# Gate columns of two hybrid mixers made in a strand of their own, five accumulators for the first head, and RMS norms summed per token

## The chip, the core and the metric

The kernel runs on one core of a Trainium2 chip. The metric is the device time of one execution in microseconds (us); a kernel's time is the median over its runs.

## What is computed

A stack of six blocks on one sequence of 512 tokens ("l") of width 1024, with a context of 256 tokens ("c") beside it in the first layer. First a two-layer network: layer 0 has a mixer (a scan and a spatial gate) and a convolutional ffn, layer 1 an mLSTM and an ffn. Then two hybrid mixers. Everything is float32. Each block begins with an RMS norm over the 1024 channels of a token. In the reference, cut to what matters here:

```python
def rms_norm(x, w):
    xf = x.astype(jnp.float32)
    y = xf * lax.rsqrt(jnp.mean(xf * xf, axis=-1, keepdims=True) + EPS)
    return (y * w.astype(jnp.float32)).astype(x.dtype)

def hybrid_mixer(h, ...):
    proj = h @ w_in
    qkv, z_a, a_lg, b_lg, cf_val, cf_glu, z_b, gate_lg = jnp.split(proj, pts, axis=-1)
    qkv = jax.nn.silu(depthwise_conv_centred(qkv, qkv_conv_w))     # 5 taps
    ...
    g = -jnp.exp(a_log) * jax.nn.softplus(a_lg + dt_bias)          # 2 directions x 4 heads
    beta = jax.nn.sigmoid(b_lg)
    o_fwd = gated_delta_chunked(q, k, v, g[:, :, 0], beta[:, :, 0])
    ...                                                            # the same backward
    y_a = (o_fwd + o_bwd, normed, times silu(z_a)) @ w_dn_out
    y_b = (a 31-tap convolution of cf_val * sigmoid(cf_glu), normed, gated) @ w_cf_out
    y = gate[:, :, 0] * y_a + gate[:, :, 1] * y_b
    return y @ w_out

for l in range(DEPTH):
    x = x + hybrid_mixer(rms_norm(x, norm_w[l]), ...)
```

`gated_delta_chunked` needs, for each head, direction and chunk of 64 tokens, the cumulated g, its exponentials and beta. These few numbers per token are the "gate columns" of the title.

## The kernel before

Activations are held channel-major: a tile is 128 channels by 512 tokens, eight tiles (KD = 8) make the width. A gemm (`gemm_tile`, `mmacc`) takes the weights in slabs of 128 output channels and runs three matmuls per input tile (L344, L347, L348: high times high, high times low part, low times high), 24 per slab of 128, into one PSUM bank. On ScalarE (L80) and VectorE (L81) each slab's weights are split into the two parts, `wh` and `wl`. A set of banks and buffers is an `Env`: its `mm` list is the accumulators that gemms take in turn, its `ps` list the banks of all else.

The norms. `normed` runs six times: at the start, before the first ffn, before the mLSTM, before the second ffn, before hybrid 0 and before hybrid 1. Where a block's output y has to be added first (the second to the fifth), it norms y, adds it to x tile by tile (L476, L470), squares each new x tile on ScalarE (L395), and sums the squares over channels on TensorE. `wide_sum` (L425) does this with one matmul per tile: a 128x128 weight of ones, the 512 tokens moving, so that every row of the bank holds the sums of all tokens. `wide_rms` reads the diagonals of that bank with one VectorE instruction per 128 tokens (L433, each with a read of its accumulator), adds epsilon (L435), raises to the power -1/2 on GpSimd (L437), and spreads the result over 128 rows by four transposes (L388). Only then can VectorE write the normed tiles (L492, L485) that the next gemm reads. Records on TensorE come in twos for a float32 matmul: the 16 records of L425 in a norm are 8 tiles.

A hybrid mixer. `hybrid` first makes the 16 gate rows by a gemm (`gate_rows`, weights `gwh`), then the gate columns, then runs `gdn_proj` for heads 0 and 1: for each head four gemms in the order k, q, v, za, each into the next accumulator of `pro`, which has banks 0, 1 and 2. After each of k, q and v, VectorE adds four taps from the bank (L1794, after ScalarE's centre tap L1786); for k and q, ScalarE squares the result (`qsq`, L2017) and TensorE sums it (L374). za is a plain gemm with a silu. The fourth gemm of a head takes the first accumulator again. Heads run as background strands, generators that the main program steps by planned times ("due"): `head(a)` waits until its head's projections are there, then yields through `gdn_head`. The strands share TensorE with the gemms that follow: `cf_proj`, heads 2 and 3, the gate and z projections, the branch 1 gemms; then `K.drain()` runs out whatever is left of the heads, and the branch 0 gemms end the mixer. Within the planned order, the final order of each engine is set by a scheduler that simulates the program while it is built.

The lines that matter below: gate columns in L1814 to L1852 (`G` L1438, exponent and logarithm L1470 to L1472, L1819, L1820, the scan L1825, the transposes L1459, `eglT` L1849), projections L2003 to L2026, a head's chain L2124 to L2160, its output transposes L2188. In the changed kernel most helper lines come 2 or 3 earlier (L344 is L342, L374 is L372, L388 is L386, L1459 is L1456, L1794 is L1791) and those of `gdn_head` 9 later.

## Time and profile before

| | |
|---|---|
| median of 3 runs | 3421.62 us (3419.37 to 3433.52) |
| profiled execution | 3418.44 us, of which 3416.7 us are the span of the trace |
| TensorE (PE) busy | 3151.7 us, 92% of the span |
| VectorE (DVE), ScalarE (ACT), GpSimd (POOL) busy | 62%, 37%, 18% |
| mean granted TensorE clock | 0.953 of full speed |

The span runs from the first to the last instruction of the core. The granted clock is the share of full TensorE speed (2.4 GHz) that the chip gave: 1.00 is 2.4 GHz, 0.50 is 1.2 GHz, values between are stretches with both. PEld is TensorE's weight loading, which overlaps its matmuls (PE). A row of a timeline reads: start in us, duration in us, engine, line, operation, what is written <- what is read, partitions and shape, how many in the row, and in brackets how long the engine had been idle before and what released it. A row of waits reads: who waited, for whom, us in total, times, longest.

### The profile page before, as it was taken

The numbers are of one execution on the slowest core, as the hardware profiler recorded it, in microseconds if no ns is written. First come the engines' busy times: TensorE is split into PE (matmuls) and PEld (weight loads), VectorE is DVE, ScalarE is ACT, GpSimd is POOL, SyncE is SP. The second block draws the span as 40 slices with busy tenths as digits, with TensorE's granted clock in tenths as the row PEclk, the third lists the DMA queues.
The fourth block names the chain that finished last, engine by engine and source line by source line (L and its number), as shares of the span: only waits on it lengthen the run. The fifth ranks groups of instructions, "written<-read, shape, count | busy, mean of one in ns | idle before, by whom it ended". The sixth has DMA issues, their size and how long they took to land.

```text
span 3416.7 us, 61935 instructions
## 1 busy us (share of the span) xinstructions
PE 3151.7 (92%) x25042; PEld 2476.2 (72%) x25042; DVE 2122.4 (62%) x4318; ACT 1269.4 (37%) x2679; POOL 614.0 (18%) x762
## 2 busy tenths in 40 slices
PE   7999898888899999989888999988999899999988
PEld 4878676667688888868765888767667567766756
DVE  4444565645855555685666576677777666677665
ACT  4333343333432222364433332352433335233332
POOL 4111222211000000010010000005156000525500
PEclk8999998999999999999998999989999899999979
DMA  6432554431222222122222223232232343123332
GB/s 228 141 94 70 166 167 155 139 112 52 73 72 68 72 73 97 57 73 69 81 78 82 91 87 132 78 99 78 69 103 95 104 138 102 57 69 108 102 115 90
DMA packets 313570, 336.10 MB, mean 98 GB/s; under 512 B 26542, under 2 KB 259132, under 8 KB 313284
## 3 DMA queue, kind: packets, MB, share of 16 engines
q1 hardware_dynamic: 311172, 329.69, 30.0%
q8 instruction: 197, 3.23, 0.4%
q0 software_dynamic: 2112, 2.45, 0.3%
q14 instruction: 89, 0.73, 0.1%
HBM read 282.13 MB, written 49.94 MB: 97 GB/s over the span
## 4 chain that ended last, share of the span: by engine, by line
PE 61%; issue 18%; DVE 14%; ACT 3%; DMA 3%; POOL 0%; SPq 0%; DVEq 0%; POOLq 0%; ACTq 0%
PE mm L344 14%; PE mm L347 13%; PE mm L348 13%; DVE cfa L1794 3%; PE ps L739 2%; PE ps L748 2%; PE ps L1192 2%; DVE wl L81 2%; PE ps L1137 1%; PE ps L558 1%; PE ps L1719 1%; PE ps L2133 1%; DMA ld<-sp 1%; PE ps L2160 1%; PE ps L1701 1%
## 5 line engine op out<-in xcount | busy, mean ns | idle before, releaser
L344 PE MATMUL mm<-hl,wh 128*128 128x512 f32 (+1 forms) x3296 | 1249.6, 383 | 56.0 <-DVE qkv L1794 15.2
L347 PE MATMUL mm<-hl,wh 128*128 128x512 f32 (+1 forms) x3296 | 1225.8, 372 | 1.6 <-DVE hl L487 1.6
L348 PE MATMUL mm<-hl,wl 128*128 128x512 f32 (+1 forms) x3296 | 1218.5, 372 | 0.0
L344 PEld LDWEIGHTS mm<-hl,wh 128*128 128x128 f32 x3296 | 631.1, 192 | 192.8 <-issue 33.2
L348 PEld LDWEIGHTS mm<-hl,wl 128*128 128x128 f32 x3296 | 631.4, 192 | 114.6 <-issue 2.8
L347 PEld LDWEIGHTS mm<-hl,wh 128*128 128x128 f32 x3296 | 633.2, 192 | 106.3 <-DVE hl L487 3.4
L80 ACT ACTIVATE wh<-wr 128x512 fp32r<-128x512 f32 (+3 forms) x718 | 367.9, 561 | 704.2 <-PE mm L347 614.3
L81 DVE TENSOR_TENSOR wl<-wr,wh 128x512 fp32r<-128x512 f32 (+3 forms) x718 | 435.7, 640 | 230.1 <-ACT wh L80 205.2
L1372 DVE SCALAR_TENSOR_TENSOR cv<-mm,vecs,cv 128x441 f32<-128x441 f32 (+2 forms) x352 | 242.9, 692 | 94.3 <-ACT cv L1360 88.2
L1423 POOL MEMSET gwh<- 128x1024 f32 x3 | 2.9, 955 | 969.2 <-PE mm L347 969.2
L1794 DVE SCALAR_TENSOR_TENSOR cfa<-ld,vecs,cfa 128x497 f32<-128x497 f32 (+14 forms) x160 | 162.1, 1013 | 13.2 <-ACT cfa L1788 11.0
L1962 POOL TENSOR_SCALAR tap<-ld,vecs 128x498 f32<-128x498 f32 (+4 forms) x80 | 150.6, 1882 | 63.9 <-PE ps L2046 29.8
L1395 DVE TENSOR_TENSOR fy<-fy,mm 128x512 f32<-128x512 f32 x96 | 55.2, 577 | 126.3 <-PE mm L348 125.5
L1963 POOL TENSOR_TENSOR cfa<-cfa,tap 128x498 f32<-128x498 f32 (+4 forms) x80 | 112.1, 1401 | 5.3
L743 ACT ACTIVATE pad<-ps 128x256 f32<-128x256 f32 (+1 forms) x100 | 46.7, 468 | 155.5 <-PE ps L739 155.0
L2138 ACT ACTIVATE u<-ps,beT 64x128 f32<-64x128 f32 x128 | 46.2, 362 | 131.3 <-DVE u L2137 130.6
L1374 ACT ACTIVATE cv<-cv,vecs 128x256 f32<-128x256 f32 (+1 forms) x66 | 43.0, 652 | 132.1 <-DVE cv L1372 77.2
L749 DVE TENSOR_TENSOR cut<-cut,ps 128x256 f32<-128x256 f32 x120 | 49.3, 413 | 54.0 <-PE ps L748 53.2
L2137 DVE TENSOR_SCALAR u<-ps,kdT 64x128 f32<-64x128 f32 x128 | 44.5, 349 | 58.4 <-PE ps L2133 44.4
L1378 DVE TENSOR_TENSOR cv<-cv,mm 128x512 f32<-128x512 f32 x66 | 39.5, 599 | 65.5 <-ACT cv L1374 36.2
L425 PE MATMUL ps<-sq,one 128*128 128x512 f32 (+1 forms) x132 | 62.6, 609 | 15.8 <-ACT sq L395 13.7
L731 POOL TENSOR_TENSOR pad<-L,zm 128x512 f32<-128x512 f32 x40 | 54.4, 1360 | 113.4 <-PE ps L739 84.0
(479 smaller groups left out, 4418.9 us busy)
## 6 DMA issues: line engine op xcount, KB each, us to landing
...
```

Source lines behind the costliest of these rows:

```text
L80: nc.scalar.activation(h[:, q:e], src, AF.Copy)
L81: nc.vector.tensor_tensor(l[:, q:e], src, h[:, q:e].bitcast(F32), SUB)
L344: mm = nc.tensor.matmul(ps[:m, :n], wh[:, i, :m], H[:, :n], start=first and i == 0, stop=False)
L347: nc.tensor.matmul(ps[:m, :n], wh[:, i, :m], L[:, :n], start=False, stop=False)
L348: nc.tensor.matmul(ps[:m, :n], wl[:, i, :m], H[:, :n], start=False, stop=last and i == nk - 1)
L739: nc.tensor.matmul(ps[r, u * 64:u * 64 + 64], L[r, u], W[r, u], start=True, stop=True)
L748: nc.tensor.matmul(ps[r, u * 64:u * 64 + 64], X[r, u], Z[r, u], start=True, stop=True)
L1192: nc.tensor.matmul(ps[hs[h], d], lhsT(d, h), rhs(d, h), start=first and i == 0 and d == 0, stop=last and i == len(parts) - 1, skip_group_c ...
L1372: nc.vector.scalar_tensor_tensor(t3[:, ro, co], a3[:, ri, ci], tap(ky, kx, ff), t3[:, ro, co], MUL, ADD)
L1794: nc.vector.scalar_tensor_tensor(dst[:, a:b], src[:, a + o:b + o], taps[j], dst[:, a:b], MUL, ADD)
L1962: nc.gpsimd.tensor_scalar(x[:, a:b], src[:, a + o:b + o], taps[j], None, MUL)
L1963: nc.gpsimd.tensor_tensor(g[:, a:b], g[:, a:b], x[:, a:b], ADD)
```

## The change

Three things. (1) `wide_sum` becomes `token_sum`: each squared tile is the weight, 128 tokens at a time, and a single column of ones moves, so the bank gets one column of sums per 128 tokens, four matmuls (eight records) per 512-token tile. `wide_rms` becomes `token_rms`: one VectorE instruction reads these columns; the power and the four transposes stay. The constant `one2` goes. (2) In `hybrid` the gate columns become a generator in a background strand with banks 6 and 7, stepped at planned times; the heads wait for `cols` too. (3) Head 0's projections run with five accumulators, banks 0, 1, 2, 4 and 5; from head 1 on it is `pro` with three.

```diff
-    def wide_sum(self, ps, t, n, first, last):
-
-        self.nc.tensor.matmul(ps[:, :n], self.one2, t[:, :n], start=first, stop=last)
+    def token_sum(self, ps, t, n, first, last):
+
+        for i in range(n // P):
+            self.nc.tensor.matmul(ps[:, i:i + 1], t[:, i * P:(i + 1) * P], self.ones, start=first and i == 0,
+                                  stop=last, skip_group_check=True)
         self.free(t)
 
-    def wide_rms(self, ps, n):
-
-        c = self.tiny([P, n // P], name="dg")
-        for i in range(n // P):
-            junk = self.s128(name="junk")
-            self.line(self.nc.vector.scalar_tensor_tensor(junk, ps[:, i * P:(i + 1) * P], 1.0 / D, self.ident, MUL, MUL,
-                                                          accum_out=c[:, i:i + 1]))
-        self.line(self.nc.vector.tensor_scalar(c, c, EPS, None, ADD))
-        r = self.tiny([P, n // P], name="rs")
-        self.nc.gpsimd.tensor_tensor(r, c, self.mhalf[:, :n // P], ALU.pow)
+    def token_rms(self, ps, n):
+
+        nch = n // P
+        v = self.tiny([P, nch], name="var")
+        self.line(self.nc.vector.tensor_scalar(v, ps[:, :nch], 1.0 / D, EPS, MUL, ADD))
+        r = self.tiny([P, nch], name="rs")
+        self.nc.gpsimd.tensor_tensor(r, v, self.mhalf[:, :nch], ALU.pow)
         return self.bcast_rows(r, n)
...
     pg = gate_rows(K, X, ONLY_L, w, 2048, 16)
-    G = K.p2(name="G")
-    scan_order(K, G, pg["l"], n, 0, gb)
...
+    cols = {}
+
+    def gate_columns():
+
+        G = K.p2(name="G")
+        scan_order(K, G, pg["l"], n, 0, gb)
...
+        ben = natural(K, G[64:128, :], n, AF.Sigmoid, 1.0)
+        yield 0, 10400
+        gcT = columns(K, [(gcn, n)], "gcT")
+        ngT = columns(K, [(egn, n)], "egT")
+        yield 900, 400
+        beT = columns(K, [(ben, n)], "beT")
+        bkT = columns(K, [(kdn, n)], "kdT")
...
+        yield 900, 0
...
+        cols["all"] = gcT, ngT, beT, bkT, eglT, gcd, egd
...
-            while h not in pre:
-                yield 0, 2000
-            yield from gdn_head(K, CH, l, h, *pre.pop(h), gcT, ngT, beT, bkT, eglT, gcd, egd, Ya, pads)
+            while h not in pre or not cols:
+                yield 0, 1000
+            yield from gdn_head(K, CH, l, h, *pre.pop(h), *cols["all"], Ya, pads)
...
+    K.background(Env([], [6, 7], [], range(24, 28)), gate_columns())
+
+    K.env = Env([0, 1, 2, 4, 5], [3], [], range(16, 24))
     for h in range(2):
         proj(h)
         K.background(heads[h], head(h), slow=SLG)
+        K.env = pro
```

How this moves instructions shows at three places. First TensorE at the norm before hybrid 0, the end of the ffn's gemm and the sums; before:

```order
L347 MATMUL mm_3480_21642<-hl_3452_21401,wh_3478_21636 128x512
L348 MATMUL mm_3480_21642<-hl_3451_21400,wl_3479_21637 128x512
L425 MATMUL ps_3496_21704<-sq_3497_21705,one2_3_79 128x512
L425 MATMUL ps_3496_21704<-sq_3504_21726,one2_3_79 128x512
L388 MATMUL ps_3511_21741<-ident_1_72,rs_3510_21739 128x128 x4
L425 MATMUL ps_3512_21746<-sq_3513_21750,one2_3_79 128x512
```

and now, from the same place:

```order
L345 MATMUL mm_3441_21682<-hl_3413_21441,wh_3439_21676 128x512
L346 MATMUL mm_3441_21682<-hl_3412_21440,wl_3440_21677 128x512
L424 MATMUL ps_3457_21744<-ones_2_77,sq_3458_21745 128x1 x4
L424 MATMUL ps_3457_21744<-ones_2_77,sq_3465_21769 128x1 x4
L386 MATMUL ps_3468_21779<-ident_1_72,rs_3467_21777 128x128 x4
L424 MATMUL ps_3469_21784<-ones_2_77,sq_3470_21788 128x1 x4
```

The two sums of y (ps_3496 before, ps_3457 now), the transposes of the scale and the first x tile's sum stand in the same order; each single L425 is four L424, the squared tile standing as the weight and `ones` as what moves.

Second, TensorE in hybrid 0, where head 0's gemms change over: mm_3606 is v, mm_3612 za, nat_... are gate rows being turned into columns. Before:

```order
L348 MATMUL mm_3606_22106<-hl_3547_21841,wl_3605_22101 128x512
L1459 MATMUL ps_3573_21949<-ident_1_72,nat_3568_21932 128x64 x4
L344 MATMUL mm_3606_22106<-hl_3550_21847,wh_3604_22100 128x512
L347 MATMUL mm_3606_22106<-hl_3551_21848,wh_3604_22100 128x512
L348 MATMUL mm_3606_22106<-hl_3550_21847,wl_3605_22101 128x512
L344 MATMUL mm_3612_22147<-hl_3529_21806,wh_3610_22141 128x512
L347 MATMUL mm_3612_22147<-hl_3530_21807,wh_3610_22141 128x512
L348 MATMUL mm_3612_22147<-hl_3529_21806,wl_3611_22142 128x512
L344 MATMUL mm_3612_22147<-hl_3532_21811,wh_3610_22141 128x512
L347 MATMUL mm_3612_22147<-hl_3533_21812,wh_3610_22141 128x512
```

Now mm_3553 is za and mm_3560 is k of head 1. The first piece is their border, the second some 20 rows on, where mm_3572, q of head 1, begins:

```order
L345 MATMUL mm_3553_22156<-hl_3504_21902,wh_3551_22150 128x512
L346 MATMUL mm_3553_22156<-hl_3503_21901,wl_3552_22151 128x512
L342 MATMUL mm_3560_22194<-hl_3482_21860,wh_3558_22188 128x512
L345 MATMUL mm_3560_22194<-hl_3483_21861,wh_3558_22188 128x512
L346 MATMUL mm_3560_22194<-hl_3482_21860,wl_3559_22189 128x512
L342 MATMUL mm_3560_22194<-hl_3485_21865,wh_3558_22188 128x512
L345 MATMUL mm_3560_22194<-hl_3486_21866,wh_3558_22188 128x512
```

```order
L342 MATMUL mm_3560_22194<-hl_3503_21901,wh_3558_22188 128x512
L372 MATMUL ps_3530_22033<-ones_2_77,qsq_3529_22031 128x1 x4
L345 MATMUL mm_3560_22194<-hl_3504_21902,wh_3558_22188 128x512
L346 MATMUL mm_3560_22194<-hl_3503_21901,wl_3559_22189 128x512
L342 MATMUL mm_3572_22254<-hl_3482_21860,wh_3570_22248 128x512
L345 MATMUL mm_3572_22254<-hl_3483_21861,wh_3570_22248 128x512
L346 MATMUL mm_3572_22254<-hl_3482_21860,wl_3571_22249 128x512
L342 MATMUL mm_3572_22254<-hl_3485_21865,wh_3570_22248 128x512
L345 MATMUL mm_3572_22254<-hl_3486_21866,wh_3570_22248 128x512
L346 MATMUL mm_3572_22254<-hl_3485_21865,wl_3571_22249 128x512
L1456 MATMUL ps_3573_22261<-ident_1_72,nat_3526_21997 128x64 x4
L1456 MATMUL ps_3575_22268<-ident_1_72,nat_3525_21994 128x64 x4
```

Before, the gate columns' transposes (L1459) stood inside the v and za gemms of head 0, and the sums of head 0's k (L374) behind them; now all four gemms of head 0 run without either, the sums of k (L372) stand near the end of head 1's k, and the transposes (L1456) in head 1's q.

Third, VectorE in the same stretch, where qkv_3587 is k of head 0 reading bank mm_3586, qkv_3597 is q, and g and gc belong to the gate columns. Before:

```order
L1819 SCALAR_TENSOR_TENSOR g_3561_21913<-G_3559_21904,lpe_3560_21909 64x512
L1794 SCALAR_TENSOR_TENSOR qkv_3587_22015<-mm_3586_21990,vecs_3491_21694,qkv_3587_22015 128x511
L1794 SCALAR_TENSOR_TENSOR qkv_3597_22073<-mm_3596_22048,vecs_3491_21694,qkv_3597_22073 128x511
L1820 TENSOR_SCALAR g_3561_21913<-g_3561_21913,al_3554_21862 64x512
L81 TENSOR_TENSOR wl_3618_22180<-wr_3616_22177,wh_3617_22179 128x512
L1794 SCALAR_TENSOR_TENSOR qkv_3587_22015<-mm_3586_21990,vecs_3491_21694,qkv_3587_22015 128x511
L81 TENSOR_TENSOR wl_3618_22180<-wr_3616_22177,wh_3617_22179 128x512
L1794 SCALAR_TENSOR_TENSOR qkv_3597_22073<-mm_3596_22048,vecs_3491_21694,qkv_3597_22073 128x511
L1825 SCALAR_TENSOR_TENSOR gc_3562_21916<-rst_22_204,g_3561_21913 64x256 x2
L81 TENSOR_TENSOR wl_3633_22248<-wr_3631_22245,wh_3632_22247 128x512
L1794 SCALAR_TENSOR_TENSOR qkv_3587_22015<-mm_3586_21990,vecs_3491_21694,qkv_3587_22015 128x510
```

and now, with qkv_3528 as k (bank mm_3517) and qkv_3538 as q:

```order
L1820 SCALAR_TENSOR_TENSOR g_3520_21981<-G_3518_21972,lpe_3519_21977 64x512
L1791 SCALAR_TENSOR_TENSOR qkv_3528_22024<-mm_3517_21968,vecs_3452_21734,qkv_3528_22024 128x511
L1791 SCALAR_TENSOR_TENSOR qkv_3538_22082<-mm_3537_22057,vecs_3452_21734,qkv_3538_22082 128x510
L1821 TENSOR_SCALAR g_3520_21981<-g_3520_21981,al_3507_21916 64x512
L1791 SCALAR_TENSOR_TENSOR qkv_3528_22024<-mm_3517_21968,vecs_3452_21734,qkv_3528_22024 128x511
L81 TENSOR_TENSOR wl_3559_22189<-wr_3557_22186,wh_3558_22188 128x512
L1791 SCALAR_TENSOR_TENSOR qkv_3538_22082<-mm_3537_22057,vecs_3452_21734,qkv_3538_22082 128x511
L81 TENSOR_TENSOR wl_3559_22189<-wr_3557_22186,wh_3558_22188 128x512
L1826 SCALAR_TENSOR_TENSOR gc_3521_21984<-rst_21_202,g_3520_21981 64x256 x2
L1791 SCALAR_TENSOR_TENSOR qkv_3528_22024<-mm_3517_21968,vecs_3452_21734,qkv_3528_22024 128x510
```

In both, the last row shown is the fourth tap of k; one tap of q and one half-split of weights (L81) that stood ahead of it now stand behind it. The scan of the gate columns is still ahead of it.

The scheduler's order also shifts by single rows in other parts of the program, without a pattern.

## Rows read from the trace of the kernel before

**Rows 1.** The page: busy time of TensorE, and the chain that ended last, by engine.
```profile
PE 3151.7 (92%) x25042; PEld 2476.2 (72%) x25042; DVE 2122.4 (62%) x4318; ACT 1269.4 (37%) x2679; POOL 614.0 (18%) x762
...
PE 61%; issue 18%; DVE 14%; ACT 3%; DMA 3%; POOL 0%; SPq 0%; DVEq 0%; POOLq 0%; ACTq 0%
```

**Rows 2.** Waits of TensorE in hybrid 0, 2236 to 2812 us.
```profile
PE mm L344 <- DVE qkv L1794: 7.6, 1, 7.6
PE ps L2188 <- DVE ot L2183: 4.8, 2, 3.0
```

**Rows 3.** Waits of TensorE in hybrid 1 and after it, 2812 to 3417 us.
```profile
PE ps L2188 <- DVE ot L2183: 5.9, 2, 3.1
```

**Rows 4.** Timeline of TensorE at the stall of hybrid 0.
```profile
2268.45 0.79 PE L344 MATMUL mm<-hl,wh 128*128 128x512 f32 x1 [7.55 <-DVE qkv L1794]
...
2273.30 0.63 PE L348 MATMUL mm<-hl,wl 128*128 128x512 f32 x1
...
2274.95 0.39 PE L348 MATMUL mm<-hl,wl 128*128 128x512 f32 x1
```

**Rows 5.** Timeline of TensorE at the stall of hybrid 1.
```profile
2849.53 0.79 PE L344 MATMUL mm<-hl,wh 128*128 128x512 f32 x1 [7.64 <-DVE qkv L1794]
```

**Rows 6.** Timeline of VectorE in the same stretch of hybrid 0.
```profile
2261.05 0.68 DVE L1819 SCALAR_TENSOR_TENSOR g<-G,lpe 64x512 f32<-64x512 f32 x1 [1.19 <-ACT lpe L1472]
...
2265.89 1.25 DVE L1825 TENSOR_TENSOR_SCAN gc<-rst,g 64x256 f32<-64x256 f32 x2
...
2267.66 0.73 DVE L1794 SCALAR_TENSOR_TENSOR qkv<-mm,vecs,qkv 128x510 f32<-128x510 f32 x1
```

**Rows 7.** Timeline of ScalarE there: head 0's first square.
```profile
2271.83 0.63 ACT L2017 ACTIVATE qsq<-qkv 128x512 f32<-128x512 f32 x1
```

**Rows 8.** Timeline of all engines at the norm before hybrid 0.
```profile
2216.49 0.29 DVE L433 SCALAR_TENSOR_TENSOR junk<-ps,ident 128x128 f32<-128x128 f32 x1 [0.81 <-PE ps L425]
...
2217.72 1.03 POOL L437 TENSOR_TENSOR rs<-dg,mhalf 128x4 f32<-128x4 f32 x1 [11.58 <-DVE dg L435]
...
2221.42 0.74 DVE L476 SCALAR_TENSOR_TENSOR fy<-fy,gp,ps 128x512 f32<-128x512 f32 x1
...
2222.68 0.74 DVE L476 SCALAR_TENSOR_TENSOR fy<-fy,gp,ps 128x512 f32<-128x512 f32 x1
```

**Rows 9.** Timeline of TensorE: that norm's wide sums.
```profile
2222.22 9.55 PE L425 MATMUL ps<-sq,one 128*128 128x512 f32 x16 [2.76 <-ACT sq L395]
```

**Rows 10.** Timeline of TensorE: the norm before the first ffn, to its first gemm.
```profile
873.42 9.98 PE L425 MATMUL ps<-sq,one 128*128 128x512 f32 x18 [1.45 <-ACT sq L395]
...
889.24 0.74 PE L344 MATMUL mm<-hl,wh 128*128 128x512 f32 x2 [0.17 <-ACT hl L497]
```

**Rows 11.** One line's instructions: L364 on VectorE.
```profile
L364 DVE TENSOR_SCALAR var<-ps x26: 150/157/163, 254.9 to 3250.4; 128x4 f32<-128x4 f32 x22, 128x2 f32<-128x2 f32 x4
```

**Rows 12.** Timeline of TensorE: L374 at 2.4 GHz.
```profile
253.93 0.95 PE L374 MATMUL ps<-ones,sq 128*128 128x1 f32 x8
```

**Rows 13.** Timeline of TensorE: L374 at 1.2 GHz.
```profile
3248.56 1.84 PE L374 MATMUL ps<-ones,sq 128*128 128x1 f32 x8 [0.68 <-DVE sq L405]
```

**Rows 14.** Busy time by stretch of 3 or 4 us, and the granted clock (PEclk).
```profile
core 0: us, PE busy (x) PEld busy (x) DVE busy (x) ACT busy (x) POOL busy (x), PEclk, DMA share, GB/s
2222.00:2226.00 4.00, 3.78 (x5) 1.67 (x6) 4.00 (x8) 2.06 (x4) 0.00 (x0) 0.50 0.52 199
2226.00:2229.00 3.00, 3.00 (x8) 1.25 (x7) 3.00 (x6) 1.26 (x2) 0.00 (x0) 0.93 0.56 218
3274.00:3277.00 3.00, 3.00 (x17) 1.84 (x16) 0.96 (x3) 0.54 (x2) 0.00 (x0) 0.50 0.00 0
...
3280.00:3283.00 3.00, 3.00 (x8) 2.32 (x9) 0.34 (x1) 0.67 (x2) 0.00 (x0) 0.50 0.00 0
3283.00:3286.00 3.00, 2.97 (x17) 1.51 (x17) 1.26 (x5) 0.37 (x2) 0.00 (x0) 0.74 0.00 0
```

More of the change, by code (lines that the diff above doesn't have):

```diff
@@ L450, in both @@
             acc = self.sumsq(tiles[:-1], s, n)
-            self.wide_sum(ps, acc, n, True, False)
-            self.wide_sum(ps, self.square(tiles[-1], s, n), n, False, True)
+            self.token_sum(ps, acc, n, True, False)
+            self.token_sum(ps, self.square(tiles[-1], s, n), n, False, True)
         if y is not None:
@@ L459, in normed @@
             for s, n in segs:
-                ry[s] = self.wide_rms(py[s], n)
+                ry[s] = self.token_rms(py[s], n)
         def sums(s, n):
@@ L471, in rest @@
                 self.free(y[s][k])
-                self.wide_sum(px[s], self.square(x[s][k], s, n), n, k == 0, k == KD - 1)
+                self.token_sum(px[s], self.square(x[s][k], s, n), n, k == 0, k == KD - 1)
             for k in range(KD):
@@ L1813, in hybrid @@
     pg = gate_rows(K, X, ONLY_L, w, 2048, 16)
-    G = K.p2(name="G")
-    scan_order(K, G, pg["l"], n, 0, gb)
-    scan_order(K, G, pg["l"], n, 64, gb)
-    l1 = softplus_neg(K, G[0:64, :], "l", n)
-    g = K.p2(name="g")[0:64]
-    nc.vector.scalar_tensor_tensor(g, G[0:64, :], 0.0, l1, MAX, ADD)
-    nc.vector.tensor_scalar(g, g, al, None, MUL)
-    K.free(l1)
-    gc = K.p2(name="gc")[0:64]
-    for x in range(2):
-        q = slice(256 * x, 256 * x + 256)
-        nc.vector.tensor_tensor_scan(gc[:, q], CH.rst[0:64], g[:, q], 0.0, MUL, ADD)
@@ L1837, in hybrid @@
-    gcT = columns(K, [(gcn, n)], "gcT")
-    ngT = columns(K, [(egn, n)], "egT")
-    beT = columns(K, [(ben, n)], "beT")
-    bkT = columns(K, [(kdn, n)], "kdT")
-    gcd, egd = [K.out_dram(t, n, 64) for t in (gcn, egn)]
-    K.free(gc, G, ben, kdn)
-    nc.vector.tensor_scalar(ngT, ngT, -1.0, None, MUL)
-    nc.vector.tensor_tensor(bkT, bkT, beT, MUL)
-    ps = K.ps()
-    for d in range(2):
-        for h in range(4):
-            o = (4 * d + h) * 8
-            nc.tensor.matmul(ps[:, o:o + 8], K.ident[:64, 32 * d + h:32 * d + h + 1].to_broadcast([64, P]), egl,
-                             start=True, stop=True)
@@ L1851, in hybrid @@
-    eglT = K.sm.tile([P, 8, 8], F32, tag="cols", bufs=8, name=K.nm("eglT"))
-    nc.vector.tensor_copy(eglT, ps[:, :64].rearrange("p (r c) -> p r c", r=8))
+    cols = {}
+    def gate_columns():
+        G = K.p2(name="G")
+        scan_order(K, G, pg["l"], n, 0, gb)
+        scan_order(K, G, pg["l"], n, 64, gb)
+        l1 = softplus_neg(K, G[0:64, :], "l", n)
+        g = K.p2(name="g")[0:64]
+        nc.vector.scalar_tensor_tensor(g, G[0:64, :], 0.0, l1, MAX, ADD)
+        nc.vector.tensor_scalar(g, g, al, None, MUL)
+        K.free(l1)
+        gc = K.p2(name="gc")[0:64]
+        for x in range(2):
+            q = slice(256 * x, 256 * x + 256)
+            nc.vector.tensor_tensor_scan(gc[:, q], CH.rst[0:64], g[:, q], 0.0, MUL, ADD)
+        c3 = "p (c i) -> p c i"
+        gl = gc.rearrange(c3, i=C64)[:, :, C64 - 1:C64]
+        egl = K.tiny([64, 8], name="egl")
+        nc.scalar.activation(egl, gl.rearrange("p c i -> p (c i)"), AF.Exp)
+        tmp = K.p2(name="tmp")[0:64]
+        nc.vector.tensor_tensor(tmp.rearrange(c3, i=C64), gl.to_broadcast([64, 8, C64]), gc.rearrange(c3, i=C64), SUB)
+        kdn = natural(K, tmp, n, AF.Exp, 1.0)
+        K.free(tmp, g)
+        egn = natural(K, gc, n, AF.Exp, 1.0)
+        gcn = natural(K, gc, n, AF.Copy, 1.0)
+        ben = natural(K, G[64:128, :], n, AF.Sigmoid, 1.0)
[5 more added lines that the diff above has]
+        bkT = columns(K, [(kdn, n)], "kdT")
+        gcd, egd = [K.out_dram(t, n, 64) for t in (gcn, egn)]
+        K.free(gc, G, ben, kdn)
+        nc.vector.tensor_scalar(ngT, ngT, -1.0, None, MUL)
+        nc.vector.tensor_tensor(bkT, bkT, beT, MUL)
+        yield 900, 0
+        ps = K.ps()
+        for d in range(2):
+            for h in range(4):
+                o = (4 * d + h) * 8
+                nc.tensor.matmul(ps[:, o:o + 8], K.ident[:64, 32 * d + h:32 * d + h + 1].to_broadcast([64, P]), egl,
+                                 start=True, stop=True)
+        eglT = K.sm.tile([P, 8, 8], F32, tag="cols", bufs=8, name=K.nm("eglT"))
+        nc.vector.tensor_copy(eglT, ps[:, :64].rearrange("p (r c) -> p r c", r=8))
+        cols["all"] = gcT, ngT, beT, bkT, eglT, gcd, egd
```

15 lines of the change are left out of this document (1 added, 14 removed).

## The prediction

> **What bounds the kernel now.** I read the page first: TensorE is busy 92% of the span, and it holds 61% of the chain that ended last, VectorE 14% [rows 1]. So a change pays only where TensorE stands still or runs at its lower clock, and it costs wherever it gives TensorE more to do on the path. I then read the waits of TensorE in each hybrid. Each has one long wait of a gemm (L344) for VectorE's convolution taps (L1794), 7.6 us [rows 2, 5], besides 4.8 and 5.9 us at the output transposes of the heads (L2188) [rows 2, 3]. The timelines place the long ones: after the v gemm of head 0, the za gemm stands 7.55 us in hybrid 0 and 7.64 us in hybrid 1 [rows 4, 5]. za is the fourth gemm, wants the first accumulator again, and that is freed by the fourth tap of k, which on VectorE runs at 2267.66 for 0.73 us [rows 6], just ahead of the gemm's start at 2268.45. Ahead of that tap VectorE does the gate columns (g waiting 1.19 us on ScalarE's logarithm, then the scan, 1.25 us) [rows 6]. The wait has a tail: the 12 matmuls from 2268.45 to 2273.30 are 0.43 us apart, those after it 0.23 (a row of 0.63 us there, 0.39 us from 2274.95) [rows 4]: the lower clock, 12 x 0.195 = 2.3 us. Together a stall of 7.6 + 2.3 = 9.9 us per hybrid.
>
> Last I read the norms, where TensorE has only its sums to do. The x tiles come from VectorE every 1.26 us (2221.42, 2222.68) [rows 8]; TensorE follows at once, 16 records in 9.55 us [rows 9]. In that stream the clock is 0.50 from 2222 to 2226 and 0.93 from 2226 to 2229, TensorE being busy nearly all of both [rows 14].
>
> **Part 1, the five accumulators and the strand.** With banks 4 and 5 in the ring, za of head 0 takes bank 4 and does not wait for k: its 24 matmuls at 0.23 us (5.6 us) move into the old stall. The next gemm, k of head 1, wants bank 0, which the same fourth tap frees. By the order one tap (0.7 us) and one half-split (0.7 us) fewer stand ahead of it, so it is done near 2267, against 2268.39; TensorE, from the end of v at 2260.9 and 5.6 us of za, is there near 2266.5: a wait of 0.2 to 0.6 us. The next thing late is the sums of k (L372), which now stand behind 22 matmuls of head 1's k, so they are reached near 2271.7. They need k's square, which ScalarE began at 2271.83 for 0.63 us [rows 7] and does not get sooner by the change; behind its table loads I let it be done at 2273.6. That is a wait of 0.8 to 1.9 us; queued behind it are two gemm matmuls and all of q of head 1. The transposes of the gate columns (L1456) come later still, in q of head 1, with their rows long ready. The matmuls themselves are the same in number. So of 9.9 us, 1 to 2.5 return as new waits, and the gain is about 8 us per hybrid, taken as 8 since the two hybrids wait alike [rows 4, 5]; bounds 6 (a short cold stretch after the new wait) and 10 (none). Sum: -16 us. The price elsewhere: heads start later in the order by about 1.75 gemms of 24, some 9 us of TensorE's work. I cost this at nothing, as the heads have the gate, z and branch 1 gemms to run beside; counted in the order, after the convolution's norm 26 to 30 rows of each kind of chain step (L2124 to L2160) are left in both versions. If that cover fails, it is the second rival.
>
> **Part 2, what the norms save.** Per RMS of the 512 tokens VectorE now takes one instruction of 0.157 us, as L364 does [rows 11], where the power on GpSimd began 1.23 us after the first diagonal [rows 8]. With the same gap of 0.09 us ahead of GpSimd the chain is 1.23 - 0.25 = 0.98 us shorter. Nine of these lie on the path: two in each of four norms, one before hybrid 1 (its y is not normed). The norm at the start lies behind the loading of weights and counts nothing; the context's own, two per long norm, lie beside other VectorE work. Sum: -8.8 us.
>
> **Part 3, what the sums cost.** A 512-token tile was two records, now it is eight, of the form of L374: 0.95 us for eight at 2.4 GHz [rows 12], 1.84 at 1.2 GHz [rows 13], 1.8 without the last one's end. At 2.4 GHz that is below the pace of 1.26 us and hidden; at 1.2 GHz it is not. So the clock decides. Which clock the new stream gets no row shows; the nearest are stretches with TensorE full of small matmuls. From 3274 to 3277 it is busy 3.00 of 3 us at 0.50, and it stays at 0.50 until it has run gemm matmuls of 512 columns, from 3280 to 3283; then comes 0.74 [rows 14]. One column per weight is smaller than anything there, and I take it that the stream stays at 1.2 GHz.
>
> The Trainium skill ("TensorE: Matmul & The Clock Gate", "What's actually happening") says that the default state is throttled and activity releases the throttle. A stream that keeps TensorE busy should then come up as the wide sums do; the rows from 3274 to 3277 speak against counting busy time as activity, and by the rule the time would be that of the first rival.
>
> Priced at the lower clock: in the norm before hybrid 0, eight tiles take 8 x 1.8 = 14.4 us against 9.55, +4.9, and with the two RMS -2.0 the gemm starts 2.9 later. The norm before the second ffn has the same eight tiles: +2.9. In the norm before the first ffn the first gemm came 15.82 us after the first x sum (873.42 to 889.24) [rows 10]. Now TensorE has 14.4 us for eight tiles, 4 x 0.9 for half of the context's (256 tokens, half the records), four transposes (1.1 us at the lower clock, from 0.65), and 4 x 0.9 again ahead of that gemm: 22.7 us, +6.9, less 0.98 for the RMS of y (that of x is inside): +5.9. The norm before the mLSTM has the same tiles: +5.9. Before hybrid 1 only two tiles are summed, at the full clock of the gemm that went before: -1.0. Sum with part 2 inside: 2.9 + 2.9 + 5.9 + 5.9 - 1.0 = +16.6. Bounds: +10, if in the two long norms half is caught up because normed tiles pile up ahead of the gemm; +21, if those gemms, which started at the full clock, begin with the cold stretch of 2.3 us that the stall of hybrid 0 had.
>
> **The sum.** 3418.4 - 16 + 16.6 = 3419 us, made against the profiled execution, which lies 3.2 us below the median and 1.0 below the lowest of the runs shown; this is within the noise of the answer. A measurement of this kernel can tell some 0.5% (17 us) from no change.
>
> **Rival 1: the sums bring up the clock.** If the stream of token sums raises the clock as the wide ones did between 2226 and 2229 [rows 14], it lags for a few us, catches up, and only -8.8 of the norms is left: 3418.4 - 16 - 8.8 = 3394. For it: TensorE would be as busy there as before. Against it: the rows from 3274 to 3277.
>
> **Rival 2: the heads give the hybrids' gain back.** The end of a hybrid waits for heads: L2188 waited 4.8 and 5.9 us for the heads' outputs [rows 2, 3]. Heads now start later in TensorE's order. If their last chain steps do not move forward with the gemms, the 8 us saved reappear there, and with the norms at the lower clock the time is 3418.4 + 16.6 = 3435; if each trails by one such wait more (4.8 and 5.9), 3446. It decides when a head's last step stands more than 8 us behind the last branch 1 gemm. Against it: the counts of rows left are equal.
>
> **Rival 3: the stall only moves.** Were k of head 1 held as long as za was, because the gate columns' work on VectorE still stands ahead of the fourth tap, only za's 5.6 us would come forward: gain 5.6 per hybrid less the sums' wait of up to 1.9 and the cold 2.3, 1.4 x 2 = 3: 3418.4 - 3 + 16.6 = 3432.
>
> **How the numbers follow.** Chances: my sum 0.55, rival 1 0.22, rival 2 0.15, rival 3 0.08. The forecast's own range is 3408 to 3428 (bounds 6 to 10 per hybrid, +10 to +21 for the norms, not all at one end). The range that leaves out no more than 2 in 10 runs from rival 1's 3394 to 3438, past rivals 3 and 2's lower time. Faster by over 0.5% (below 3404.5 of the median 3421.6): nearly all of rival 1 and a little of mine, with the scattered shifts in the order, 0.28. Slower (above 3438.7): half of rival 2, a little of mine, 0.14. Within: 0.58.
>
> **What would show it.** In the changed kernel's trace: the waits of L342 for L1791 at 7.6 us gone in both hybrids, with a wait of 0.8 to 1.9 us at L372; a row of L424 x8 of about 1.8 us and a granted clock of 0.50 through the norms before both ffns, the mLSTM and hybrid 0; GpSimd's power some 0.25 us after the last sum. The prediction is wrong if the clock is 1.00 by the fourth tile of a norm, or if the waits of L2197 (the old L2188) grow by the 8 us saved.

## The result and the profile after

The changed kernel takes 3446.61 us (3445.89 to 3450.28, 6 runs) where the kernel before takes 3423.63 us (3419.37 to 3433.52, 6 runs): 1.0066 of it, with a 95% interval of 1.0051 to 1.0081. It is slower by 23 us; forecast were 3419 us and a range up to 3438.

The page of the changed kernel, its first lines, the chain that ended last and the group of the token sums:

```profile
span 3443.9 us, 62483 instructions
...
PE 3208.0 (93%) x25350; PEld 2559.5 (74%) x25350; DVE 2104.5 (61%) x4218; ACT 1273.5 (37%) x2682; POOL 624.1 (18%) x761
...
PE 77%; DVE 12%; ACT 4%; issue 3%; DMA 3%; POOL 1%; SPq 0%; DVEq 0%; POOLq 0%; ACTq 0%
...
L424 PE MATMUL ps<-ones,sq 128*128 128x1 f32 x440 | 86.3, 329 | 17.2 <-ACT sq L393 16.3
```

TensorE is busy 56 us longer than before and its share of the chain has grown from 61% to 77% [rows 1]; 86 us of it are the token sums (L424), 63 us were the wide ones. To see where the 27 us between the two profiled executions arose, the two timelines of TensorE are laid side by side at the first instruction of each stage:

| stretch, from its start to the next one's | before, us | after, us | longer by | forecast |
|---|---|---|---|---|
| start and mixer of layer 0, to the first sum of y | 864.1 | 880.1 | +16.0 | 0 |
| norm before the first ffn | 25.2 | 34.8 | +9.6 | +5.9 |
| first ffn | 565.0 | 563.9 | -1.2 | 0 |
| norm before the mLSTM | 23.8 | 28.6 | +4.7 | +5.9 |
| mLSTM | 333.7 | 335.8 | +2.1 | 0 |
| norm before the second ffn | 24.6 | 26.5 | +1.8 | +2.9 |
| second ffn | 377.2 | 372.8 | -4.4 | 0 |
| norm before hybrid 0 | 22.7 | 25.3 | +2.7 | +2.9 |
| hybrid 0 | 573.9 | 580.6 | +6.7 | -8 |
| norm before hybrid 1 | 7.3 | 6.8 | -0.5 | -1.0 |
| hybrid 1, to the long row of output transposes | 583.8 | 572.9 | -10.9 | -8 |

The five norms that were costed give +18.3 against +16.6. What the forecast lacked stands elsewhere: in layer 0, where only the norm at its start was edited, and in the hybrids, which together give 4 us where 16 were forecast. A hybrid's row by itself says little. From the first gemm of hybrid 0 to the last gemm of the program the changed kernel takes 1160 us, and the kernel before and the six experiments below that share its hybrids (e1, e5, e6, e7, e13, e14) take 1158 to 1167, with 578 to 588 for hybrid 0 and the norm behind it alone. So no gain of the hybrids shows in these two traces.

**The norms.** TensorE's timeline at the norm before the first ffn, which answers to [rows 10]:

```profile
883.84 4.42 PE L424 MATMUL ps<-ones,sq 128*128 128x1 f32 x20 [3.19 <-ACT sq L393]
889.75 1.54 PE L386 MATMUL ps<-ident,rs 128*128 128x128 f32 x6 [1.48 <-POOL rs L434]
893.62 17.23 PE L424 MATMUL ps<-ones,sq 128*128 128x1 f32 x80 [2.33 <-ACT sq L393]
910.71 1.09 PE L386 MATMUL ps<-ident,rs 128*128 128x128 f32 x4
911.60 3.41 PE L424 MATMUL ps<-ones,sq 128*128 128x1 f32 x16
914.87 0.77 PE L342 MATMUL mm<-hl,wh 128*128 128x512 f32 x1
```

The pause of 3.19 us at the sums of y is ScalarE's. The last squares of y are queued there behind the half-split of the ffn's first weights (L80), which waits for their DMA:

```profile
880.78 2.19 ACT L80 ACTIVATE wh<-wr 128x512 fp32r<-128x512 f32 x4 [3.24 <-DMA wr<-in_ffn_up_dram]
882.87 1.44 ACT L393 ACTIVATE sq<-yo 128x512 f32<-128x512 f32 x3
```

In e7 and e14 below, which sum y by wide sums as the kernel before does, ScalarE waits for this DMA too (3.33 and 2.11 us; 0.36 in the kernel before), and this norm takes 30.4 and 29.5 us where the kernel before takes 25.2. So a part of its +9.6 belongs to the new order of what goes before it and not to the token sums.

The 80 records (eight tiles of the tokens, four of the context) run without a pause for 17.23 us, 0.215 us a record; from the first x sum to the first gemm it is 21.25 us, where 22.7 were worked out and 15.82 stood before. The windows tell the clock (columns as in [rows 14]) in that norm and the three that follow:

```profile
core 0: us, PE busy (x) PEld busy (x) DVE busy (x) ACT busy (x) POOL busy (x), PEclk, DMA share, GB/s
901.00:905.00 4.00, 4.00 (x21) 4.00 (x20) 3.37 (x10) 2.40 (x6) 0.00 (x0) 0.50 0.64 232
1494.00:1502.00 8.00, 8.00 (x39) 8.00 (x39) 4.90 (x15) 2.62 (x7) 1.01 (x1) 0.50 0.14 52
1851.00:1859.00 8.00, 7.47 (x35) 7.47 (x36) 7.97 (x13) 4.22 (x7) 0.00 (x0) 0.50 0.52 197
2250.00:2257.00 7.00, 7.00 (x34) 7.00 (x34) 7.00 (x12) 3.42 (x6) 0.00 (x0) 0.50 0.58 224
```

TensorE and its weight loading (PEld) are busy all of the time, or nearly (7.47 of 8 us), at 0.50. Where the wide sums had come to 0.93 [rows 14], the token sums stay at 1.2 GHz to their end, in all four norms.

**Layer 0.** One window from the kernel before and one from the changed kernel, over the same stretch of the scan (the ends are matched by the gemm matmul that follows):

```profile
590.00:742.00 152.00, 127.34 (x2375) 96.83 (x2374) 86.05 (x213) 56.43 (x167) 37.30 (x62) 0.94 0.44 141
```
```profile
590.00:756.00 166.00, 141.62 (x2393) 106.02 (x2388) 86.34 (x216) 57.55 (x169) 36.74 (x62) 0.88 0.42 132
```

About the same instructions, TensorE idle for 24.7 us in the one and 24.4 us in the other, VectorE, ScalarE and GpSimd busy as long. Only the clock differs, 0.94 and 0.88, and TensorE's busy time with it, 127 and 142 us: the 14 us.

**Hybrid 0.** TensorE where the old stall was (za of head 0 now runs through, and so does k of head 1, up to its last matmuls):

```profile
2304.32 1.05 PE L372 MATMUL ps<-ones,qsq 128*128 128x1 f32 x8 [1.80 <-ACT qsq L2026]
...
2306.19 0.63 PE L342 MATMUL mm<-hl,wh 128*128 128x512 f32 x1
...
2308.33 0.56 PE L346 MATMUL mm<-hl,wl 128*128 128x512 f32 x1
...
2314.43 1.02 PE L372 MATMUL ps<-ones,qsq 128*128 128x1 f32 x8 [2.23 <-DVE beT L1459]
```

The 7.55 us of [rows 4] are gone. In their place stand a wait of 1.80 us at the sums of k, and one of 2.23 at the next sums; behind the first the gemm matmuls come 0.43 us apart again (2306.19, duration 0.63 as in the cold stretch of [rows 4]). The windows:

```profile
2306.00:2310.00 4.00, 4.00 (x17) 2.83 (x17) 1.37 (x4) 3.96 (x8) 1.01 (x1) 0.66 0.43 124
2314.00:2318.00 4.00, 3.57 (x21) 3.58 (x21) 3.42 (x10) 1.12 (x2) 1.50 (x3) 0.69 1.09 292
2318.00:2322.00 4.00, 4.00 (x13) 3.30 (x13) 0.23 (x2) 3.71 (x6) 1.80 (x4) 0.50 0.06 20
```

Low clock for (1 - 0.66) x 2 x 4 = 2.7, 2.5 and 4.0 us, 9 us in all, in which half the work is lost: 4.6 us. With the waits, 4.0, that is 8.6 of the 9.9 us that were taken away. In hybrid 1 the waits sit at the strand's own transposes:

```profile
PE ps L1456 <- DVE gcT L1459: 3.2, 1, 3.2
PE ps L1456 <- ACT nat L1444: 2.5, 1, 2.5
```

### The profile page after: what moved, and what is told of

Read it like the earlier page. It is cut to its first block, busy times and chain, and to the rows that moved or that the text cites. A ratio compares the mean times of both kernels' runs of the same rounds, so it can differ in the third digit from the quotient of the medians.

```text
span 3443.9 us, 62483 instructions
## 1 busy us (share of the span) xinstructions
PE 3208.0 (93%) x25350; PEld 2559.5 (74%) x25350; DVE 2104.5 (61%) x4218; ACT 1273.5 (37%) x2682; POOL 624.1 (18%) x761
## 4 chain that ended last, share of the span: by engine, by line
PE 77%; DVE 12%; ACT 4%; issue 3%; DMA 3%; POOL 1%; SPq 0%; DVEq 0%; POOLq 0%; ACTq 0%
PE mm L342 19%; PE mm L345 17%; PE mm L346 17%; DVE cfa L1791 3%; PE ps L736 2%; PE ps L745 2%; PE ps L1189 2%; PE ps L424 2%; DVE wl L81 2%; PE ps L1134 2%; PE ps L555 1%; PE ps L2154 1%; PE ps L2169 1%; PE ps L1716 1%; ACT wh L80 1%
## 5 line engine op out<-in xcount | busy, mean ns | idle before, releaser
L80 ACT ACTIVATE wh<-wr 128x512 fp32r<-128x512 f32 (+3 forms) x718 | 367.8, 561 | 635.2 <-PE mm L345 567.7
L81 DVE TENSOR_TENSOR wl<-wr,wh 128x512 fp32r<-128x512 f32 (+3 forms) x718 | 437.9, 644 | 262.5 <-ACT wh L80 246.5
L1791 DVE SCALAR_TENSOR_TENSOR cfa<-ld,vecs,cfa 128x497 f32<-128x497 f32 (+14 forms) x160 | 151.5, 947 | 6.2 <-ACT cfa L1785 3.8
L424 PE MATMUL ps<-ones,sq 128*128 128x1 f32 x440 | 86.3, 329 | 17.2 <-ACT sq L393 16.3
L424 PEld LDWEIGHTS ps<-ones,sq 128*128 128x128 f32 x440 | 86.1, 303 | 20.5 <-ACT sq L393 18.0
L555 PE MATMUL ps<-ar,csil 128*32 128x512 f32 x384 | 67.2, 723 | 6.3 <-DMA ar<-in_ada_w_dram 6.3
```

The source lines that it names most:

```text
L80: nc.scalar.activation(h[:, q:e], src, AF.Copy)
L81: nc.vector.tensor_tensor(l[:, q:e], src, h[:, q:e].bitcast(F32), SUB)
L424: self.nc.tensor.matmul(ps[:, i:i + 1], t[:, i * P:(i + 1) * P], self.ones, start=first and i == 0, stop=last, skip_group_check=True)
L555: m = nc.tensor.matmul(ps[32 * c:32 * c + 32, :], self.csil[:, k, :], raw[c // 2][:, 512 * (c % 2):512 * (c % 2) + 512], start=k == 0, sto ...
L1791: nc.vector.scalar_tensor_tensor(dst[:, a:b], src[:, a + o:b + o], taps[j], dst[:, a:b], MUL, ADD)
```

## The experiments

All times in us, as medians. "Before" is the kernel before, run on the same chip beside the experiments that share its number; the ratio is to it.

| run | median | before | ratio, 95% interval |
|---|---|---|---|
| e1_norms | 3449.97 | 3427.55 | 1.0058, 1.0041 to 1.0075 |
| e2_hybrid | 3424.81 | 3427.55 | 0.9984, 0.9971 to 0.9997 |
| e3_wide_first | 3439.94 | 3427.55 | 1.0030, 1.0019 to 1.0040 |
| e4_five | 3431.17 | 3427.55 | 1.0007, 0.9997 to 1.0016 |
| e5_mid_tokens | 3453.00 | 3427.62 | 1.0064, 1.0041 to 1.0087 |
| e6_keepwarm | 3499.02 | 3427.62 | 1.0210, 1.0193 to 1.0227 |
| e7_norm1 | 3452.02 | 3427.62 | 1.0069, 1.0054 to 1.0084 |
| e8_pairs | 3414.04 | 3427.62 | 0.9955, 0.9940 to 0.9970 |
| e9_change_pairs | 3434.71 | 3425.98 | 1.0027, 1.0010 to 1.0044 |
| e10_pairs_three | 3419.00 | 3425.98 | 0.9987, 0.9975 to 1.0000 |
| e11_pairs_k1 | 3414.13 | 3425.98 | 0.9965, 0.9948 to 0.9983 |
| e12_pairs_pace | 3423.97 | 3425.98 | 0.9993, 0.9983 to 1.0003 |
| e13_norm1_pad | 3445.23 | 3426.80 | 1.0052, 1.0033 to 1.0072 |
| e14_norm1_long | 3439.04 | 3426.80 | 1.0037, 1.0024 to 1.0050 |
| e15_pairs_ytok | 3409.04 | 3426.80 | 0.9954, 0.9938 to 0.9971 |

The theory after the result (A): the norms' sums lose to the low clock; the first norm's change reorders layer 0 and lowers the clock there; the hybrids' stall comes back in other places. Its main rivals: the hybrids did the damage, or something other than order slowed layer 0.

**Halves apart.** e1 takes `token_sum` and `token_rms` alone, e2 the part of the diff on `hybrid` alone.

> Only the norms are changed, the hybrids are as before. Theory A (the loss is the norms' alone: token sums run at the 1.2 GHz clock, about +19 us in four norms, and the other norm, the first, shifts the scheduler's order in layer 0's scan, +13 us): 3424 + 19 + 13 - 1 = 3455 us, with the scan from 590 to 742 us longer by 12 to 14. Rival B (the strand and the accumulators cost what the whole lost beyond the norms): 3424 + 19 = 3443 us or less, with layer 0 as long as before.

> Only the hybrids are changed (strand and five accumulators), the norms are as before. Theory A: the stalls of 7.6 us go, hybrid 1 gains 10 and hybrid 0 gives its gain back at its end, so 3424 - 5 = 3419 us, and up to layer 0's end the trace equals that of before within 1 us. The prediction's own theory: 3424 - 16 = 3408 us. Rival B: hybrid 0 loses 7 and hybrid 1 too, 3435 us or more.

The loss is the norms': +22 us, between B's +19 and A's +31 (the interval leaves A's out), with the scan late as A said (16 us, by the count of gemm matmuls used below). The hybrids' part is worth -3 us, near A's -5 and far from the -16 of the prediction. In e2's trace the stall is replaced by two waits of the strand:

```profile
PE ps L1459 <- DVE gcT L1462: 3.2, 1, 3.2
PE ps L1459 <- ACT nat L1447: 2.5, 1, 2.5
```

**The five accumulators alone**, e4:

```diff
+    K.env = Env([0, 1, 2, 4, 5], [3], [], range(16, 24))
     for h in range(2):
         proj(h)
         K.background(heads[h], head(h), slow=SLG)
+        K.env = pro
```

> Only the five accumulators, for the first head's projections; gate columns inline and norms as before. Theory A: the wait of 7.6 us of za is gone, but the heads' steps decide the end, so -2 to -8 us: 3416 to 3422. Prediction's own theory: the stall is paid by the accumulators alone, 3424 - 16 = 3408 us. Rival D (without the strand the gate columns' transposes take over the wait): the wait turns up at L1459, 3420 to 3428 us.

No gain, and neither A nor rival D had it right: the same wait, with the same length, now stands at k of head 1, and a head's first transposes wait behind za's silu.

```profile
PE mm L344 <- DVE qkv L1794: 7.6, 1, 7.6
...
PE ps L2048 <- ACT za L2027: 2.1, 1, 2.1
```

The cover that the prediction counted on was not used. In the order that the scheduler gave this program, 21 of the 24 matmuls of head 1's k stand ahead of head 0's za, and k wants bank 0, which the fourth tap frees behind the gate columns' work. So e4 tells what the accumulators do in that order; whether za's 5.6 us would have covered a part of the wait in the order forecast, as rival 3 of the prediction has it, was not tested.

**Which norms.** In e3 the whole change keeps wide sums in the first norm; in e5 only the four norms with a y take token sums; in e7 only the first.

```diff
+        tok = y is None and sh is not None          # e7; e3: not that; e5: y is not None
+        add, rms = (self.token_sum, self.token_rms) if tok else (self.wide_sum, self.wide_rms)
```

> The whole change, but the first norm (ahead of layer 0) sums as before. Theory A: layer 0's scan gets the order it had, and its 13 us come back: 3447 - 13 = 3434 us, the ffn's norm starting 16 us earlier than in the changed kernel. Rival C (the scan's 13 us have another cause, such as the constant that went or where buffers lie): 3447 us, with the scan as slow as in the changed kernel.

> Only the four norms with a y to add use token sums; the first norm, the one before hybrid 1, and the hybrids are as before. Theory A (those sums run at 1.2 GHz): four norms at +8, +7, +2 and +3 as in the changed kernel's trace, so +19 us on the kernel before, and layer 0's scan as fast as before. Rival (the loss in layer 0's scan comes with any change of the norms): +32 us.

> Only the first norm is changed to token sums. Theory A (its shorter norm makes the scheduler place the scan of layer 0 in another order, which leaves TensorE at 1.2 GHz for longer): +13 us, all between 590 and 742 us, with more time at a clock of 0.50 there and no more idle time. Rival C (the scan's 13 us come from buffers or the constant that went): as before within 3 us.

e7 by itself costs 24 us, more than A's 13, though its norm is short and lies behind the loading of weights. e3 stands 12 us over the kernel before, the changed kernel 23: the first norm's share in the whole change is some 11. e5 lost 25 instead of 19, in runs from 3438 to 3455. Its trace shows 10 us in layer 0, whose order is the same as in e3 on all engines, and there that stretch took as long as before: the 1126th gemm matmul of the program (L344, L347 and L348 counted in order of time), near the end of the scan, begins at 715.0 us in the kernel before, 715.8 in e3 and 725.5 in e5. So the scan's time also varies from one execution to another. The other norms cost about as in the changed kernel, the mLSTM's with what follows it more (+13).

**Order or token sums?** e13 puts four VectorE instructions of 128x128 into the first norm's token chain; e14 has no token sum anywhere, but reads the first norm's diagonals twice:

```diff
-        for i in range(n // P):
+        for i in [*range(n // P)] * (2 if self.longer else 1):      # e14, longer: first norm only
```

> Only the first norm by token sums, as in the run with it alone, but four (two for the context) more VectorE instructions of 128x128 stand in its chain, so that it takes as long as before. The build still gives layer 0 another order than before, and another than the token sums without them. Theory A1 (any other order of the scan than the one in the kernel before costs, since that one happened to keep the clock up): 3435 to 3452 us where the kernel before is at 3426, the first gemm after the scan 8 to 24 us late. Rival (the order that the shorter norm brings is a bad one in itself, others are as good): within 5 us of the kernel before.

> The kernel before with wide sums everywhere; only the first norm reads its diagonals twice, 1 us more of VectorE, and the scheduler again orders layer 0 anew. No token sum at all. Theory A1: 3435 to 3452 us, the scan longer at the 1.2 GHz clock. Rival F (the token sums themselves, not the order, slow layer 0): 3427 us, one more than the kernel before.

e13 lost 18 us, so the shorter norm as such is not what matters. e14 shows that no token sum is needed: with 1 us more of VectorE behind the loading of weights 12 us are lost by the median of its five runs (3430.0 to 3442.7 us, interval clear of the kernel before), and in the profiled one, the fastest of them, the 1126th gemm matmul is 11 us late (726.0). Its scan, in the same window form as above:

```profile
590.00:754.00 164.00, 141.83 (x2408) 105.70 (x2405) 87.06 (x217) 57.40 (x169) 36.98 (x63) 0.89 0.43 136
```

TensorE idle 22.2 us, less than before, and a clock of 0.89. In five profiles with token sums in the first norm (the changed kernel, e1, e7, e9, e13) that matmul begins between 729.0 and 738.9 us; in eleven whose order on TensorE up to there is that of the kernel before (in e3, e5 and e6 but for the last 65 rows), up to 725.5, ten of them by 719.8. So another order of the same instructions is enough to leave TensorE at 1.2 GHz for longer. For the place of the loss in e14 there is one trace, hardly later than the latest of the eleven. Which feature of these orders does it, or whether the buffers do that an order takes, was not found.

**Can the clock be kept up?** e6 is e5 with one more wide matmul, read by nobody, ahead of each x tile's token sum:

```diff
+                nc.tensor.matmul(spare[:, :n], self.one2, sq[:, :n], start=True, stop=True)
                 add(px[s], sq, n, k == 0, k == KD - 1)
```

> The same, and ahead of each token sum of an x tile one more matmul of 128x512 whose result nobody reads (2 more records, 0.43 us each at 1.2 GHz, 0.23 at 2.4). Theory A (the moving 512-column matmuls bring the clock up and single columns don't): the clock goes to 1.00 within four tiles, a tile then takes 0.95 + 0.46 = 1.4 us, and the four norms cost about as much as without the extra work or less, +10 to +20 us in all. Rival (busy time decides, or the weight loads hold the clock down): the clock stays at 0.50, a tile takes 1.8 + 0.86 = 2.7 us, and each norm ends 7 us later still, +45 us or more.

A was wrong here: +71 us, the rival's case. Rows of the norm before the first ffn, and a window over all of it:

```profile
880.18 2.07 PE L492 MATMUL ps<-sq,one 128*128 128x512 f32 x2 [2.33 <-ACT sq L395]
882.04 1.71 PE L443 MATMUL ps<-ones,sq 128*128 128x1 f32 x8
883.61 2.06 PE L492 MATMUL ps<-sq,one 128*128 128x512 f32 x2
```
```profile
880.00:906.00 26.00, 25.82 (x73) 17.56 (x74) 10.93 (x22) 6.17 (x12) 0.00 (x0) 0.50 0.27 101
```

Wide and token sums alternate, 1.85 and 1.6 us apart, TensorE busy 25.8 of 26 us, half of it with 512 columns moving, and the clock is 0.50 to the end. The wide sums alone came to 0.93 [rows 14], the token sums alone stayed at 0.50, and so did both in turn.

**The strand's own wait.** A strand has banks 6 and 7 for four sets of transposes, so the third waits until VectorE has copied the first out. e8 (norms as before) and e9 (the whole change) put two sets into one bank:

```diff
-        gcT = columns(K, [(gcn, n)], "gcT")
-        ngT = columns(K, [(egn, n)], "egT")
+        two = columns(K, [(gcn, n), (egn, n)], "gcT")
+        gcT, ngT = two[:, 0:4], two[:, 4:8]
```

(and so for beT and bkT).

> The hybrids changed as in the changed kernel, norms as before, and the gate columns' four transposes put two to a bank, so that the second pair doesn't wait for VectorE's copy out of the first. Theory A (the strand's own wait for its banks, 2 to 3 us and the low clock behind it, 3 to 5 us, takes back most of the stall's gain): the waits of the transposes for VectorE's copy are gone, and each hybrid gains 3 to 6 us on the version without pairs, so 3412 to 3420 us. Rival D (the gain is given back at the heads' end whatever happens here): 3425 us as without pairs.

> The whole change, with the gate columns two to a bank. Theory A (the pairs take the strand's own wait away whatever the norms do): 10 to 13 us less than the changed kernel, 3434 to 3437 us where the kernel before is at 3424, and about 10 over it. Rival (in the changed kernel the hybrids already had the order that the pairs bring): as the changed kernel within 3 us.

e8 takes 13.6 us off the kernel before, 0.9955 of it; without the pairs it was 3. In e9 the changed kernel loses 9 us instead of 23. Both times are as A said. In e8's first stretch of hybrid 0:

```profile
PE mm L344 <- DVE qkv L1794: 3.0, 1, 3.0
PE ps L1856 <- DVE gcT L1462: 2.0, 1, 2.0
PE mm L344 <- ACT hl L495: 1.5, 1, 1.5
PE ps L374 <- DVE kq L2033: 1.5, 1, 1.5
```

The transposes (L1459) wait no more; 3.0 us at k of head 1, 2.0 at `eglT` (L1856) and 1.5 at the sums of k are left. The gain is not in the waits, though. All of hybrid 0 and the norm behind it, in e2 and in e8:

```profile
2241.51:2826.03 584.52, 543.78 (x3739) 405.58 (x3739) 401.11 (x748) 222.35 (x438) 189.10 (x135) 0.92 0.31 97
2237.20:2812.30 575.10, 532.83 (x3739) 397.86 (x3739) 395.91 (x746) 222.97 (x438) 188.67 (x135) 0.94 0.31 98
```

TensorE is idle for 40.7 us in e2 and 42.3 in e8; what fell by 11 us is the busy time of the same 3739 records, at a clock of 0.94 instead of 0.92. The pairs also change the order, and how much of this follows from the wait that went and how much from the order was not separated.

**What is left.** e10 is e8 with `pro` for both heads, e11 lets head 1's projections begin with bank 5 (`Env([5, 0, 1, 2], ...)`), e12 has `SLG = 0.9`, which makes the heads' steps due earlier.

> Norms as before, strand with pairs, but three accumulators for both heads, so that the za gemm of head 0 waits for k's fourth tap again. Theory A (pairs and strand alone free VectorE, the accumulators give a gemm's length of cover, 5.6 us): the wait of L344 for L1794 is 5 to 8 us, and 3418 to 3424 us, 4 to 10 more than with five accumulators. Rival (five accumulators do nothing, as they did alone): as the pairs with five, 3414 us.

> Norms as before, strand with pairs, and head 1's projections begin with bank 5, so that k of head 1 doesn't wait for head 0's taps. Theory A: its wait of 3.0 and 3.2 us goes, and 3 to 6 us in all are gained if they aren't given back: 3408 to 3412 us. Rival D (what is gained at a hybrid's start is given back at its end, where the heads' steps stand): 3414 us as without.

> Norms as before, strand with pairs, and the heads' planned times shortened by a tenth (0.9 for 1.0), which puts their steps earlier into TensorE's order. Theory A (of the 13 us that a hybrid gains at its start 6 to 9 are given back at its end because the heads trail): less is given back from the last 200 gemm matmuls on, and 3405 to 3412 us. Rival E (earlier steps wait for VectorE in the middle and lower the clock there): waits of L2169 and L2157 grow, 3414 to 3425 us.

e10: with three accumulators the wait is back, and half of the gain is gone: 7 us under the kernel before instead of 13.6. So the five are worth some 7 us once the strand and the pairs are there, and nothing alone (e4).

```profile
PE mm L344 <- DVE qkv L1794: 8.6, 1, 8.6
```

e11: the 3.0 us at k are gone, `eglT` waits longer instead, and the time is that of e8:

```profile
PE ps L1856 <- DVE gcT L1462: 4.6, 1, 4.6
```

e12 is only 2 us under the kernel before. Windows from 2320 to 2815 us of e8, then of e12:

```profile
2320.00:2815.00 495.00, 459.19 (x3374) 338.46 (x3373) 346.59 (x653) 172.05 (x363) 181.43 (x123) 0.93 0.30 97
```
```profile
2320.00:2815.00 495.00, 458.10 (x3342) 340.42 (x3341) 343.68 (x633) 166.57 (x354) 173.86 (x122) 0.90 0.30 93
```

As busy, and at a clock of 0.90 instead of 0.93: the time and the clock are rival E's. Of the two waits that it named, L2169's grew from 10.6 to 12.8 us and L2157's fell from 4.6 to 3.7. The heads' steps did move forward, as A has it: the 8201st to the 8400th gemm matmul, near the end of hybrid 0, take 47.5 us where e8 has 72.4. But what goes before them in hybrid 0 takes 507 us instead of 467.

**Token sums where TensorE is still warm.** e15 is e8 with token sums for y and before hybrid 1 only, right behind a gemm.

> Hybrids with strand, five accumulators and pairs; token sums only where they follow a gemm at once, for the y of four norms and before hybrid 1; wide sums for the x tiles and in the first norm. Theory A (those few sums run at 2.4 GHz and cost nothing, and each RMS is 0.98 us shorter): 5 x 0.98 = 5 us less than the pairs alone, 3407 to 3411 us, with layer 0 as before. Rival (the shorter chain is lost again to another order of what follows): 3414 us or more.

The fastest median, 3409.04 us, 0.9954 of the kernel before; e8 has 0.9955, so the 5 us are not shown. In the traces the five norms, each from the end of the gemm ahead to the start of the gemm behind, take 103.4 us in all, and 104.8 in e8. Either version beats both kernels: by 0.5% the one before, by 1.1% the changed one.

## Why the prediction was wrong

Forecast were 3419 us, and 3446.6 were measured. The norms' sums cost what they were priced at. What failed are two terms that were put at nothing, the first norm (5) and the heads' later start (2), and a step of part 1 (1).

1. **Part 1, the stall.** Right that za no longer waits, and that the sums of k take over a wait of 0.8 to 1.9 us (1.80). The step that failed is "The transposes of the gate columns (L1456) come later still, in q of head 1, with their rows long ready": in e2 and in hybrid 1 of the changed kernel they wait 2.5 us for ScalarE's rows and 3.2 for VectorE's copy out of their first bank, two banks serving four sets. And the cold stretch, which only the lower bound had, came behind the new waits: 4.0 us of waits and 4.6 us of lost clock in hybrid 0, against 1 to 2.5. At the stall the gain was near 1 us there, not 8. With the banks paired and the rest of the hybrids' change the same (e8), the kernel gains 13.6 us.
2. **"I cost this at nothing"** for the later heads, and rival 2, whose mechanism is there in both hybrids. From the 8201st to the 8401st gemm matmul, near the end of hybrid 0, and from the 9505th to the 9728th, near the end of hybrid 1, first the kernel before, then the changed one:

```profile
2718.53:2782.43 63.90, 60.12 (x269) 43.91 (x268) 41.41 (x95) 23.95 (x60) 2.70 (x3) 0.95 0.48 158
3203.28:3340.10 136.82, 120.12 (x906) 83.81 (x905) 78.46 (x188) 43.28 (x113) 32.65 (x24) 0.84 0.33 108
2746.99:2820.41 73.42, 67.03 (x299) 48.01 (x298) 46.23 (x108) 25.25 (x64) 3.73 (x5) 0.88 0.45 144
3217.57:3366.22 148.65, 128.45 (x1000) 89.88 (x999) 84.49 (x194) 45.45 (x116) 38.87 (x29) 0.82 0.32 101
```

The same gemm matmuls now take 10 and 12 us longer, with 30 and some 95 more of the heads' matmuls among them. All kernels above with the strand and `SLG = 1.0` agree (72.3 to 75.0 and 146.8 to 148.7 us), and so do all without it (63.5 to 65.2 and 136.1 to 138.6). In e2 hybrid 0 was 8 us ahead of the kernel before at the first of these places and 3 behind after the second. Equal counts behind the convolution's norm did not show this, nor did the sign that the prediction had named: L2197 waits 0.4 and 3.3 us where the old L2188 waited 4.8 and 5.9. Rival 2's 3435 us and the first norm's 11 (e3) add up to the measured time; that it fits to the microsecond is luck, as single stretches vary by more.
3. **Part 2** (0.98 us per RMS): GpSimd's power follows the sums as forecast, at the norm before the first ffn 0.30 us after VectorE's first instruction (888.38 and 888.68) where it was 1.23 [rows 8]. The norm before hybrid 1, which has nothing else, gained 0.5 instead of 1.0.
4. **Part 3**, the likeliest case at the low clock, was right in mechanism and sum: +18.3 against +16.6. The term that was small is the norm before the first ffn, +9.6 against 5.9: its sums of y, costed at nothing, wait 3.19 us for a square, behind ScalarE's wait for a DMA, and then run cold (20 records in 4.42 us), 4.2 us more than before.
5. **"The norm at the start lies behind the loading of weights and counts nothing"** is the step that cost most. Its own instructions do count nothing, but it moves the scheduler's simulated times, and the scan behind it was ordered anew: +14 us in the profile, some 11 of the whole 23 (e3), 24 us by itself (e7), 12 us with no token sum at all (e14). The text ahead of the prediction has the order shift "by single rows in other parts of the program, without a pattern". That is wrong: up to the 1126th gemm matmul some 600 of TensorE's 5300 matmuls stand in another place than before. The prediction gave such shifts no more than a little of its range.
